# First k-tiles of each later norm multiplied before the token's factor is known (two-layer decoder trunk, one core)

## The chip, the core and the metric

The kernel runs on one core of a Trainium2 chip. Five engines work on their own queues: TensorE (PE, matmuls, with its weight loads shown as PEld), VectorE (DVE), ScalarE (ACT), GpSimd (POOL) and SyncE (SP, which here issues every DMA). The metric is the device time of one execution in microseconds, and each kernel's time is the median of several runs.

## The reference

The model has two layers over 256 tokens of width 2048. Each layer is a mixer and a squared-ReLU MLP. Both begin with an RMS norm that a conditioning vector scales and shifts. Cut to what the change touches:

```python
mod = cond @ ada_w[l] + ada_b[l]
sh1, sc1, g1, sh2, sc2, g2 = [m[:, None, :] for m in jnp.split(mod, 6, axis=-1)]
h = rms_norm(x, norm1_g[l]) * (1.0 + sc1) + sh1
x = x + g1 * mixer(h)                      # layer 0: mLSTM and retention, layer 1: sparse attention
h = rms_norm(x, norm2_g[l]) * (1.0 + sc2) + sh2
x = x + g2 * (jnp.square(jax.nn.relu(h @ mlp_w1[l])) @ mlp_w2[l])
```

`rms_norm` divides each token by the root of the mean of its squares. So for a token t and a weight column, `h @ W` is r[t] times the sum over k of x[t,k] a[k] W[k], plus the sum over k of sh[k] W[k], where r[t] is the token's factor, a = gain x (1 + scale), and the second sum is the same for all tokens.

## The kernel before, in words

Everything is float32 at the ends. Inside, a matmul is made from split operands: `wsplit` rounds a weight tile to `wh` on ACT (line 224) and puts the rest into `wl` on DVE (line 225), and an activation tile `hs` holds its rounded part in columns 0 to 255 and the rest in 256 to 511. One product is then wh x high, wh x rest, wl x high: `tmul` (line 240) does it in two matmuls of 512 and 256 columns, `nmul2` (line 273) in three of 256.

The activations are kept transposed: `xT` has 16 k-tiles of 128 features by 256 tokens. `linear` (line 245) walks over the k-tiles of one group of up to 512 weight columns: for each pair of k-tiles it loads and splits the weights, calls `fill` (below), and multiplies tile by tile into one PSUM bank per entry of its plan; after the last k-tile each entry is evacuated. `residual` (line 455) does the output projections: two groups of eight columns of `xT` each, whose evacuation (line 465, DVE) adds the gated result to `xT[:, k, :]` and tells the next `Norm` with `add(k)`. In the final steps of a group the last `stag` k-tiles are multiplied together, so that the tiles end one after another.

PSUM has eight banks of 512 float32 columns: four in rotation under the name `L` (`lbank`), four single ones M0 to M3 (`bank(i)`). The MLP's first product takes its banks from a rotation over seven (`banks1`), M3 is left to side work. SBUF pools rotate too: 16 `hs` tiles, four each of `raw`, `wh` and `wl`, three `half` tiles of 128x256.

There are four norms. The first is made at the start of the kernel in another way. The three later ones stand at three borders: mixer to MLP in layer 0, MLP to attention input between the layers, attention to MLP in layer 1. There `Norm.add` squares each finished k-tile on ACT (line 419), DVE adds up the first twelve (line 423), and `finish` (line 431) sums over the features with matmuls against ones: the accumulated tile and the last four squares, which gives the sum for every token in all 128 partitions. Then come sqrt (438, ACT), reciprocal (440, DVE) and one Newton step (178 to 180, DVE) over 128x256, and for each of the 16 k-tiles a multiply by the gain column and the factor (447, DVE), the shift with rounding (449, ACT) and the rest (450, DVE). The first matmul behind the border needs the first of these tiles.

Conditioning sums for later norms are worked in beside the matmuls: `Fill(chunks, slots)` has 32 rows of `ada_w` per chunk (line 373 loads one, 375 and 377 multiply and add on DVE) and spreads them evenly over its calls, one per step of `linear`. `side` runs one queued piece of other work per tile.

The order on each engine is made by a list scheduler: the text's order is the priority, an instruction is taken when its inputs and a buffer are there, and `tc.high_priority(offset=n)` moves a block n instructions ahead in priority (60 for the weight splits). On the chip each queue runs in the order that came out.

## Time and profile before

| | us |
|---|---|
| median of 3 runs (lowest, highest) | 2402.22 (2401.34, 2403.44) |
| the profiled execution | 2399.19 |
| its span, first to last instruction | 2397.4 |
| PE busy | 2307.6 (96%) |
| DVE busy | 1720.2 (72%) |
| ACT busy | 1189.9 (50%) |
| POOL busy | 0.5 (0%) |
| mean granted TensorE clock | 0.985 |
| DMA, mean over the span | 255 GB/s |

Rows of a timeline give the start and the length in us, the engine, the line, the operation with output and inputs, and a count; brackets give the idle time of the engine ahead of it and what ended it. Rows of waits give the waiting engine and line, what it waited for, the total, the number of waits and the longest. Rows of groups give busy us and the mean in ns behind the bar. `L124` is the helper that issues every matmul; `L`, `M` in a row are PSUM banks. A granted clock of 0.5 is half speed of PE.

### The profile page before, as it was taken

Reading aid. Unit: us, or ns where it says so; the run is one execution under the profiler, and the core shown is the slowest. Engines: PE = TensorE matmul, PEld = TensorE weight load, DVE = VectorE, ACT = ScalarE, POOL = GpSimd, SP = SyncE. Lnnn points to the kernel's source line nnn. Section 1 sums busy time; section 2 is a strip of 40 time slices with the busy share of each in tenths; the row PEclk is TensorE's granted clock in tenths of the full one; section 3 lists DMA queues with packets and bytes.
Section 4 is the critical chain, followed back from the end, with each engine's and each line's share of the span. In section 5 each row is a group of like instructions: output and inputs, shape, how many; then the busy total and the mean of one; then the engine's idle time right before and its main releaser. Section 6 shows DMA issues by size and latency. Waiting matters only on the chain.

```text
span 2397.4 us, 37302 instructions
## 1 busy us (share of the span) xinstructions
PE 2307.6 (96%) x14101; PEld 2046.1 (85%) x14101; DVE 1720.2 (72%) x2479; ACT 1189.9 (50%) x2205; POOL 0.5 (0%) x8
## 2 busy tenths in 40 slices
PE   5899999999899999999999899999999999999999
PEld 3688889998788888899899799998887888888887
DVE  6768889987877778877877877766676545555545
ACT  3235544444555556555544445755554555544442
POOL 0000000000000000000000000000000000000000
PEclk8999999999999999999999999999999999999999
DMA  9998889988799899888888675444787666565554
GB/s 332 367 291 294 286 292 327 334 295 290 242 322 310 291 316 312 285 307 293 293 311 299 219 254 142 141 140 151 245 307 238 188 184 191 192 193 194 193 193 158
DMA packets 268908, 611.96 MB, mean 255 GB/s; under 512 B 26692, under 2 KB 95286, under 8 KB 268728
## 3 DMA queue, kind: packets, MB, share of 16 engines
q1 hardware_dynamic: 268728, 609.59, 76.6%
q8 instruction: 110, 1.80, 0.3%
q14 instruction: 70, 0.57, 0.1%
HBM read 607.38 MB, written 2.12 MB: 254 GB/s over the span
## 4 chain that ended last, share of the span: by engine, by line
PE 77%; DVE 9%; DMA 9%; issue 3%; ACT 2%; SPq 1%; DVEq 0%; ACTq 0%
PE L L124 46%; PE M L124 30%; DMA ada<-in_ada_w_dram 7%; DVE wl L225 3%; DVE acc L658 1%; DVE acc L377 1%; DMA raw<-in_even_w_in_dram 1%; PE M L317 1%; ACT wh L224 1%; SPq L235 0%; DVE cv L968 0%; ACT junk L320 0%; DVE xT L465 0%; DVE sc L1179 0%; DMA xn<-in_x_dram 0%
## 5 line engine op out<-in xcount | busy, mean ns | idle before, releaser
L124 PE MATMUL L<-hs,wh 128*128 128x256 f32 (+1 forms) x4672 | 1172.8, 328 | 21.1 <-ACT hs L449 7.7
L224 ACT CAST wh<-raw 128x1024 fp32r<-128x1024 f32 (+2 forms) x736 | 765.4, 1042 | 853.6 <-PE M L124 464.0
L225 DVE TENSOR_TENSOR wl<-raw,wh 128x1024 fp32r<-128x1024 f32 (+2 forms) x736 | 887.0, 1211 | 412.9 <-ACT wh L224 402.9
L124 PE MATMUL L<-hs,wl 128*128 128x256 f32 (+1 forms) x3184 | 900.1, 283 | 6.3 <-DVE wl L225 6.2
L124 PEld LDWEIGHTS L<-hs,wh 128*128 128x128 f32 x4672 | 787.0, 191 | 97.7 <-ACT hs L449 8.1
L124 PEld LDWEIGHTS L<-hs,wl 128*128 128x128 f32 (+1 forms) x3184 | 607.2, 191 | 9.3 <-DVE wl L225 7.5
L124 PE MATMUL M<-hs,wh 128*128 128x512 f32 (+2 forms) x1816 | 541.0, 355 | 0.5 <-DVE half L310 0.5
L377 DVE SCALAR_TENSOR_TENSOR acc<-ada,cond,acc 128x1024 f32<-128x1024 f32 x300 | 384.5, 1282 | 149.2 <-DMA ada<-in_ada_w_dram 148.1
L124 PE MATMUL M<-hs,wl 128*128 128x256 f32 (+1 forms) x1476 | 415.2, 281 | 0.0
L124 PEld LDWEIGHTS M<-hs,wh 128*128 128x128 f32 (+1 forms) x1816 | 318.4, 188 | 60.4 <-issue 1.4
L124 PEld LDWEIGHTS M<-hs,wl 128*128 128x128 f32 (+1 forms) x1476 | 278.9, 189 | 1.5 <-issue 0.8
L124 PE MATMUL L<-wh,hs 128*128 128x512 f32 x640 | 210.6, 390 | 0.0
L124 PE MATMUL M<-wh,hs 128*128 128x512 f32 x560 | 185.1, 389 | 0.0
L124 PEld LDWEIGHTS L<-wh,hs 128*128 128x128 f32 x640 | 120.2, 188 | 25.1 <-PE M L124 0.3
L124 PE MATMUL L<-wl,hs 128*128 128x512 f32 x320 | 124.8, 390 | 0.0
L124 PEld LDWEIGHTS M<-wh,hs 128*128 128x128 f32 x560 | 105.1, 188 | 22.0
L124 PE MATMUL M<-wl,hs 128*128 128x512 f32 x280 | 108.9, 389 | 0.0
L320 ACT ACTIVATE junk<-M 128x128 f32<-128x128 f32 x210 | 55.2, 279 | 90.8 <-PE M L317 90.5
L658 DVE SCALAR_TENSOR_TENSOR acc<-ar,cond,acc 128x512 f32<-128x512 f32 x120 | 90.2, 751 | 4.6 <-DMA ar<-in_ada_w_dram 0.9
L556 ACT ACTIVATE half<-half 128x256 f32<-128x256 f32 x128 | 51.5, 413 | 70.7 <-DVE half L310 70.4
L206 ACT CAST hs<-z 128x256 fp32r<-128x256 f32 x192 | 76.2, 400 | 9.7 <-PE L L124 9.7
L207 DVE TENSOR_TENSOR hs<-z,hs 128x256 fp32r<-128x256 f32 x192 | 79.0, 418 | 2.2 <-ACT hs L206 2.2
(247 smaller groups left out, 1299.2 us busy)
## 6 DMA issues: line engine op xcount, KB each, us to landing
raw<-in_mlp_w_dram SPq DMA_DIRECT2D x512, 512.0 KB, 4.5
ada<-in_ada_w_dram SPq DMA_DIRECT2D x320, 512.0 KB, 5.9
raw<-in_even_w_in_dram SPq DMA_DIRECT2D x136, 256.0 KB, 5.5
ar<-in_ada_w_dram SPq DMA_DIRECT2D x64, 512.0 KB, 7.9
raw<-in_odd_w_in_dram SPq DMA_DIRECT2D x48, 512.0 KB, 3.7
raw<-in_even_w_out_dram SPq DMA_DIRECT2D x32, 512.0 KB, 5.8
raw<-in_odd_w_out_dram SPq DMA_DIRECT2D x32, 512.0 KB, 3.7
raw<-in_even_w_in_dram SPq DMA_DIRECT2D x28, 512.0 KB, 5.3
```

The source lines that it names most:

```text
L124: PE.matmul(o, a, b, start=start, stop=stop, skip_group_check=True)
L206: S.copy(h[:, 0:T], src)
L207: V.tensor_tensor(h[:, T:2 * T], src, h[:, 0:T].bitcast(F32), op=OP.subtract)
L224: S.copy(wh[:, :n], raw[:, :n])
L225: V.tensor_tensor(wl[:, :n], raw[:, :n], wh[:, :n].bitcast(F32), op=OP.subtract)
L317: PE.transpose(b[:, i * P:(i + 1) * P], t, ident)
L320: S.activation(j, b[:, i * P:(i + 1) * P], func, accum_out=dst[:, i:i + 1])
L377: V.scalar_tensor_tensor(acc, r, cond[:, kr:kr + 1], acc, op0=OP.mult, op1=OP.add)
L556: S.activation(a, a, AF.Relu)
L658: V.scalar_tensor_tensor(acc, ar[:, kr], cc, acc, op0=OP.mult, op1=OP.add)
```

## The change

At each of the three borders `finish` is replaced. Norm, in `add`, now has DVE sum all 16 squares (and the pool of squares has three tiles instead of five). The stage behind the border begins with a new function `entry`, which takes the place of the first group of the MLP (four tiles of 128 columns, group 0 of 16) or of the first `linear` of attention (key, value, index key and index weight columns).

`entry` first calls `plain`: for the k-tiles 0 to 7 it makes tiles `u` that hold gain times `xT` without the token's factor, split into a high part and a rest, and between them two columns with the high part and the rest of the shift. The `hs` tiles are two columns wider for that. `umul` multiplies such a tile in three matmuls of 258, 256 and 258 columns, so that columns 256 and 257 of the bank collect the shift's products.

`lengths` (priority 600 instructions ahead) gets the token's factor: two matmuls with the accumulated squares as stationary operand and one column of ones give the sums with tokens in partitions, 128x2; sqrt, reciprocal and Newton step run on 128x2; `spread` puts the factor on a diagonal and a matmul with ones brings it to 128x256, which ACT copies to SBUF as `rb`.

The k-tiles 8 to 15 are normed as before (`normed`) and multiplied into two other banks (`late`, two tiles each). After the loop the k-tiles 0 to 7 are normed too, for the groups that follow. Then each of the four tiles is evacuated: the held unscaled sum times `rb` (DVE), the two shift columns added (ACT copy, DVE), and the late sum plus both (DVE). The four held sums are in M0, M1, M2 and an `L` bank in the MLP, in four `L` banks in attention; the late sums in two `L` banks or in M0 and M1.

The slots over which two of the fills are spread change: from 100 to 88 for the first (three chunks, layer 0's mixer), from 100 to 70 for the last (one chunk, layer 1's MLP).

```diff
     def hs_tile():
-        return hsp.tile([P, 2 * T], F32R, tag="hs", name="hs")
+        return hsp.tile([P, 2 * T + 2], F32R, tag="hs", name="hs")
...
+        def plain(self, l, n):
             sh = shift(l, 3 * n)
+            s2 = small.tile([P, 8, 2], F32R, tag="sh2", bufs=1, name="sh2")
+            S.copy(s2[:, :, 0], sh[:, 0:8])
+            V.tensor_tensor(s2[:, :, 1], sh[:, 0:8], s2[:, :, 0].bitcast(F32), op=OP.subtract)
+            us = []
+            for k in range(8):
+                u, a = hs_tile(), acol[:, l, n, k:k + 1]
+                S.activation(u[:, 0:T], xT[:, k, :], AF.Copy, scale=a)
+                S.copy(u[:, T:T + 2], s2[:, k, :].bitcast(F32))
+                V.scalar_tensor_tensor(u[:, T + 2:], xT[:, k, :], a, u[:, 0:T].bitcast(F32), op0=OP.mult, op1=OP.subtract)
+                us.append(u)
+            return us
+
+        def lengths(self):
+            with tc.high_priority(offset=600):
+                b = bank(3)
+                for t in range(2):
+                    mm(b[:, t:t + 1], self.acc[:, t * P:(t + 1) * P], one1, start=t == 0)
+                y, v = st(2, "nv"), st(2, "nw")
+                S.activation(y, b[:, 0:2], AF.Sqrt, scale=1.0 / D, bias=epsc)
+                V.tensor_scalar(v, b[:, 0:2], 1.0 / D, EPS, op0=OP.mult, op1=OP.add)
+                V.reciprocal(y, y)
+                newton(y, v, st(2, "rs_a"))
+                self.rb = tmp.tile([P, T], F32, tag="nm", bufs=1, name="nm")
+                S.copy(self.rb, spread(y, 3))
...
+    def umul(o, u, wh, wl, c, m, start, stop):
+        mm(o[0:m, 0:T + 2], wh[:, c:c + m], u[:, 0:T + 2], start=start, stop=False)
+        mm(o[0:m, 0:T], wh[:, c:c + m], u[:, T + 2:2 * T + 2], start=False, stop=False)
+        mm(o[0:m, 0:T + 2], wl[:, c:c + m], u[:, 0:T + 2], start=False, stop=stop)
+
+    def entry(W, cols, tiles, norm, l, n, held, late, evac, fill):
+        w = sum(b - a for a, b in cols)
+        us = norm.plain(l, n)
+        norm.lengths()
+        hs = [None] * KT
+        for k0 in range(0, KT, 2):
+            if k0 == 8:
+                for k in range(8, KT):
+                    hs[k] = norm.normed(l, n, k)
+            wh, wl = wload(W, k0, 2, cols)
+            fill()
+            for q, (c, m) in enumerate(tiles):
+                for kk in range(2):
+                    k = k0 + kk
+                    if k < 8:
+                        umul(held[q], us[k], wh, wl, kk * w + c, m, k == 0, k == 7)
+                    else:
+                        nmul2(q % 2)(late[q // 2], hs[k], wh, wl, kk * w + c, m, k == 8 and q % 2 == 0, k == KT - 1)
+            side()
+        for k in range(8):
+            hs[k] = norm.normed(l, n, k)
+        for q, (c, m) in enumerate(tiles):
+            b = held[q]
+            t, s = tmp.tile([P, T], F32, tag="half", name="half"), st(1, "shs")
+            V.tensor_tensor(t[0:m], b[0:m, 0:T], norm.rb[0:m], op=OP.mult)
+            S.copy(s[0:m], b[0:m, T:T + 1])
+            V.tensor_tensor(s[0:m], b[0:m, T + 1:T + 2], s[0:m], op=OP.add)
+            evac(q, m, late[q // 2][0:m, q % 2 * T:q % 2 * T + T], s, t)
+        return hs
...
+            def evac_first(q, m, b, s, t):
+                V.scalar_tensor_tensor(t, b, s, t, op0=OP.add, op1=OP.add)
+                squared(q, t)
...
+            hs = entry(io["mlp_w1"][l], [(0, 512)], [(j * P, P) for j in range(4)], before, l, 1,
+                       [bank(0), bank(1), bank(2), lbank()], [lbank(), lbank()], evac_first, fill)
-            for g in range(DFF // 512):
+            for g in range(1, DFF // 512):
...
-        fill = Fill([(0, 2), (0, 3), (0, 4)], 100)
+        fill = Fill([(0, 2), (0, 3), (0, 4)], 88)
...
-    mlp(1, hs, Fill([(1, 5)], 100), None)
+    mlp(1, nrm, Fill([(1, 5)], 70), None)
```

More of the change, by code (lines that the diff above doesn't have):

```diff
@@ L417, in add @@
         def add(self, k):
-            s = tmp.tile([P, T], F32, tag="sq", bufs=5, name="sq")
+            s = tmp.tile([P, T], F32, tag="sq", bufs=3, name="sq")
             S.activation(s, xT[:, k, :], AF.Square)
@@ L421, in add @@
                 V.tensor_copy(self.acc, s)
-            elif self.n < KT - 4:
+            else:
                 V.tensor_tensor(self.acc, self.acc, s, op=OP.add)
-            else:
-                self.last.append(s)
             if self.n == 9:
@@ L429, in add @@
             self.n += 1
-        def finish(self, l, n):
-            b = bank()
-            mm(b[:, 0:T], ones, self.acc, start=True, stop=False)
-            for i, s in enumerate(self.last):
-                mm(b[:, 0:T], ones, s, start=False, stop=i == len(self.last) - 1)
-            y = tmp.tile([P, T], F32, tag="nm", bufs=1, name="nm")
-            v, a = (tmp.tile([P, T], F32, tag="sq", bufs=5, name="sq") for _ in range(2))
-            S.activation(y, b[:, 0:T], AF.Sqrt, scale=1.0 / D, bias=epsc)
-            V.tensor_scalar(v, b[:, 0:T], 1.0 / D, EPS, op0=OP.mult, op1=OP.add)
-            V.reciprocal(y, y)
-            newton(y, v, a)
-            rb = y
-            sh = shift(l, 3 * n)
-            hs = []
-            for k in range(KT):
-                t = tmp.tile([P, T], F32, tag="half", name="half")
-                V.scalar_tensor_tensor(t, xT[:, k, :], acol[:, l, n, k:k + 1], rb, op0=OP.mult, op1=OP.mult)
-                h = hs_tile()
-                S.activation(h[:, 0:T], t, AF.Identity, bias=sh[:, k:k + 1])
-                V.scalar_tensor_tensor(h[:, T:2 * T], t, sh[:, k:k + 1], h[:, 0:T].bitcast(F32),
-                                       op0=OP.add, op1=OP.subtract)
-                hs.append(h)
-            return hs
@@ new lines, in normed @@
+        def normed(self, l, n, k):
+            t = tmp.tile([P, T], F32, tag="half", name="half")
+            V.scalar_tensor_tensor(t, xT[:, k, :], acol[:, l, n, k:k + 1], self.rb, op0=OP.mult, op1=OP.mult)
+            h, sh = hs_tile(), shift(l, 3 * n)
+            S.activation(h[:, 0:T], t, AF.Identity, bias=sh[:, k:k + 1])
+            V.scalar_tensor_tensor(h[:, T:2 * T], t, sh[:, k:k + 1], h[:, 0:T].bitcast(F32),
+                                   op0=OP.add, op1=OP.subtract)
+            return h
@@ L534, in result, with mlp @@
                 SP.dma_start(out[0, t * P:(t + 1) * P, c * 512:(c + 1) * 512], o)
-    def mlp(l, hs, fill, norm):
+    def mlp(l, before, fill, norm):
         with ExitStack() as es:
@@ L1077, in tile_trunk @@
     mixs.close()
-    hs = nrm.finish(0, 1)
-    nrm = Norm()
-    mlp(0, hs, Fill([(0, 5), (1, 0), (1, 1), (1, 3), (1, 4)], 256), nrm)
+    before, nrm = nrm, Norm()
+    mlp(0, before, Fill([(0, 5), (1, 0), (1, 1), (1, 3), (1, 4)], 256), nrm)
     fill = Fill([(1, 2)], 60)
-    hs = nrm.finish(1, 0)
     wO = io["odd_w_in"][0]
@@ L1134, in evac_s, with evac_in @@
                 V.tensor_scalar(iw.rearrange("p a b -> p (a b)"), tb[:, 0:32], 0.25 * 0.125, None, op0=OP.mult)
-        linear(wO, KT, 2, [(2048, 2304), (3328, 3392), (3328, 3408)], hget_ := (lambda k: hs[k]),
-               [[(0, P), (P, P)], [(2 * P, P), (3 * P, 16)]], evac_s, lambda j: lbank(), fill=fill)
+        def evac_in(q, m, b, s, t):
+            V.scalar_tensor_tensor((kT, vT, ik, iwT)[q], b, s[0:m], t[0:m], op0=OP.add, op1=OP.add)
+            if q % 2:
+                evac_s(q // 2)
+        hs = entry(wO, [(2048, 2304), (3328, 3392), (3328, 3408)], [(0, P), (P, P), (2 * P, P), (3 * P, 16)],
+                   nrm, 1, 0, [lbank() for _ in range(4)], [bank(0), bank(1)], evac_in, fill)
+        hget_ = lambda k: hs[k]
         sc1 = ap.tile([P, T], F32, name="sc1")
```

18 lines of the change are left out of this document (8 added, 10 removed).

## The prediction

> **What bounds the kernel now.** I read the page's busy table first, then the waits with TensorE (PE) as the waiting engine, then the stretches around the three later norms, then the timeline there. PE is busy 96% of the span, so only what PE loses counts; ScalarE (ACT) and VectorE (DVE) matter where PE waits for them.
>
> ```profile
> PE 2307.6 (96%) x14101; PEld 2046.1 (85%) x14101; DVE 1720.2 (72%) x2479; ACT 1189.9 (50%) x2205; POOL 0.5 (0%) x8
> ...
> PE L L124 <- ACT hs L449: 7.7, 1, 7.7
> PE L L124 <- DVE hs L450: 5.7, 2, 5.0
> PE M L317 <- DVE acc L377: 5.3, 1, 5.3
> ```
>
> Two of these waits are on the normed tiles `hs` of `finish`, the third (a conditioning sum) lies inside the first border and hides the norm behind it. In stretches cut at the last residual matmul and the first matmul of the next stage (columns: length, busy time and count of PE, weight load, DVE, ACT, POOL, granted clock, DMA share, GB/s):
>
> ```profile
> 596.71:609.20 12.49, 4.66 (x19) 2.89 (x18) 12.49 (x19) 5.92 (x17) 0.00 (x0) 0.71 0.80 259
> 609.20:612.50 3.30, 3.30 (x11) 2.83 (x12) 3.30 (x9) 2.42 (x12) 0.00 (x0) 0.53 0.67 256
> 1342.27:1354.82 12.55, 3.58 (x14) 1.76 (x13) 12.08 (x22) 3.92 (x10) 0.00 (x0) 0.79 0.58 178
> 1354.82:1360.00 5.18, 5.18 (x24) 4.69 (x25) 5.18 (x14) 3.04 (x8) 0.00 (x0) 0.52 1.09 369
> 1656.14:1665.54 9.40, 3.45 (x19) 2.42 (x18) 9.21 (x15) 4.88 (x10) 0.00 (x0) 0.90 0.63 209
> 1665.54:1670.50 4.96, 4.96 (x15) 4.28 (x16) 4.96 (x13) 3.22 (x8) 0.00 (x0) 0.51 0.07 29
> ```
>
> I call the borders A (mixer to MLP, layer 0), B (MLP to attention input) and C (attention to MLP, layer 1). Each costs its gap and then a stretch at half the granted clock, in which (1 - clock) of the length is lost: A 12.49 + 3.30 x 0.47 = 14.0, B 12.55 + 5.18 x 0.48 = 15.0, C 9.40 + 4.96 x 0.49 = 11.8, together **40.9 us**. That is the most the borders can give back. DVE is busy for the whole of A's gap, 12.08 of 12.55 us at B and 9.21 of 9.40 at C; this decides the rest.
>
> The Trainium skill, "TensorE: Matmul & The Clock Gate", section "Part 1: The HAM clock gate", has PE fall to half speed after an idle window of about 3.4 us and need some 3.4 us of work to leave it. By it a resume would cost 1.7 us, 5.1 for three, and a wait below its window nothing beyond itself. A's 3.30 us agrees, B's 5.18 and C's 4.96 are longer, and the row at 587.29 below is a wait of 1.79 us that is followed by 3.30 us at clock 0.50, which goes against the window.
>
> **The change part by part.** A's timeline, PE's last residual products first:
>
> ```profile
> 595.83 0.40 PE L124 MATMUL L<-hs,wh 128*128 128x256 f32 x2
> 596.19 0.40 PE L124 MATMUL L<-hs,wh 128*128 128x256 f32 x2
> 596.43 0.28 PE L124 MATMUL L<-hs,wl 128*128 128x256 f32 x1
> 597.30 0.87 DVE L465 SCALAR_TENSOR_TENSOR xT<-L,mod,xT 128x256 f32<-128x256 f32 x2
> 600.68 1.74 DVE L440 RECIPROCAL nm<-nm 128x256 f32<-128x256 f32 x1
> 603.42 0.41 DVE L178 TENSOR_TENSOR sq<-nm 128x256 f32<-128x256 f32 x1
> 603.75 1.28 DVE L377 SCALAR_TENSOR_TENSOR acc<-ada,cond,acc 128x1024 f32<-128x1024 f32 x1
> 604.95 0.42 DVE L179 SCALAR_TENSOR_TENSOR sq<-sq 128x256 f32<-128x256 f32 x1
> 607.48 1.27 DVE L447 SCALAR_TENSOR_TENSOR half<-xT,acol,nm 128x256 f32<-128x256 f32 x3
> 609.20 0.79 PE L124 MATMUL L<-hs,wh 128*128 128x512 f32 x1 [0.65 <-DVE hs L450]
> ```
>
> *Removed:* the last eight squares no longer go into PE's sums (they did so in its idle time, so nothing is won), and the chain of sqrt, reciprocal and Newton step over 128x256 gives way to one over 128x2. *Added to PE:* eight k-tiles of unscaled products, 4 tiles each, three matmuls of 258, 256 and 258 columns per tile; nearest is the three-matmul form above, 0.36 us (595.83 to 596.19). These need only the first half of xT, which is final half a residual earlier, so PE can start at once: 8 x 4 x 0.36 = 11.5 us of work. The other eight follow, 23.0 us in all.
>
> ```profile
> 560.00:596.71 36.71, 34.92 (x278) 34.72 (x277) 26.52 (x30) 13.70 (x18) 0.00 (x0) 0.95 0.88 300
> 1300.00:1342.27 42.27, 42.27 (x271) 37.89 (x270) 26.11 (x33) 17.01 (x35) 0.00 (x0) 1.00 0.84 267
> 1620.00:1656.14 36.14, 36.14 (x303) 36.14 (x302) 17.52 (x21) 15.05 (x19) 0.00 (x0) 1.00 0.59 180
> L449 ACT ACTIVATE hs<-half,mod 128x256 fp32r<-128x256 f32 x48 | 21.1, 498 | 15.9 <-DVE half L447 15.8
> ```
>
> *Making the unscaled tiles:* eight multiply-subtracts on DVE (0.48 us each by the 128x256 rows below, 3.8 us) and on ACT eight scalings (0.50 us by L449's 128x256 row, 4 us) and eight two-column copies. DVE has 10 to 18 us free ahead of each border, ACT over 20, and the old tiles' buffers come free while the residual runs, so I cost this at nothing; without that cover it is 3.8 us of DVE per border.
>
> *The token's factor.* Five 128x2 steps and two 128x128 diagonal ones: 5 x 0.16 + 2 x 0.28 = 1.4 us of DVE, with a matmul and copies between. By estimate the squares and sums behind the last xT (598.2 at A) take 1.5 us (two of 0.42 each way, and the hand-over) and this chain 4; another DVE operation of 1.2 us can slip between its steps, as L377 does above. The factor stands between 5.5 and 10 us after PE's last residual product, bounds from no slip and from four; both are below 11.5, so PE has its first eight k-tiles and the wait that opened the borders goes.
>
> ```profile
> L178 DVE TENSOR_TENSOR rs_a<-hf 128x2 f32<-128x2 f32 (+1 forms) x51 | 7.7, 157 | 0.6
> L196 DVE TENSOR_SCALAR diag<-c,hf x2: 280/283/286, 1388.7 to 1388.9; 128x128 f32<-128x128 f32 x2
> L310 DVE TENSOR_TENSOR half<-L,half 128x256 f32<-128x256 f32 x74 | 31.0, 420 | 5.2 <-ACT half L309 3.7
> L465 DVE SCALAR_TENSOR_TENSOR xT<-L,mod,xT 128x256 f32<-128x256 f32 x48 | 21.1, 477 | 4.3 <-PE L L124 4.3
> 623.98 3.49 DVE L225 TENSOR_TENSOR wl<-raw,wh 128x1024 fp32r<-128x1024 f32 x3
> 1342.91 2.04 DVE L465 SCALAR_TENSOR_TENSOR xT<-M,mod,xT 128x256 f32<-128x256 f32 x5
> 1353.74 1.28 DVE L447 SCALAR_TENSOR_TENSOR half<-xT,acol,nm 128x256 f32<-128x256 f32 x3
> 1366.02 0.97 DVE L225 TENSOR_TENSOR wl<-raw,wh 128x800 fp32r<-128x800 f32 x1
> 1367.19 0.48 DVE L450 SCALAR_TENSOR_TENSOR hs<-half,mod,hs 128x256 fp32r<-128x256 f32 x1 [0.19 <-ACT hs L449]
> ```
>
> *What is late next.* `entry` holds four PSUM banks for the unscaled sums and two for the late ones, and lets them go only in its evacuations, which stand behind all sixteen `normed` tiles and share their three `half` buffers. Before, the next group found three free banks; now an MLP finds one and attention, which needs an `L` bank, none. So PE stops at the end of the first group until DVE has come through its list. From B's rows sixteen normed tiles take 1353.74 to 1367.67 less 0.97 and 0.19: **12.8 us**. A weight split is 3.49 / 3 = 1.16 us, the narrow one 0.97. An MLP tile's evacuation is 0.42 + 0.16 + 0.48 = 1.06 us of DVE, and a bank pair needs two. Fill rows due in the eight steps are 5.0, 4.4 and 3.8 (steps times 160/254, 32/58, 32/68); I let 3, 3 and 2 of them come ahead, at 1.28. DVE's list from PE's last residual product:
> A: last xT 0.9, two sums 0.8, factor 1.4, nine splits 10.5 (seven here, two of the next group), normed 12.8, fill 3.8, two evacuations 2.1 = 32.3 us.
> B: xT 2.4, four sums 1.7, factor 1.4, splits 7 x 0.97 + 1.2 = 8.0, normed 12.8, fill 3.8, one held bank 0.6 = 30.7.
> C: as A with two fill rows: 31.1.
> PE has 23.0 us of work, at A and C also the first tile of the next group for two steps (1.4): it waits 7.9, 7.7 and 6.7 us, and I add 2.0 for the half clock after each, the middle of the losses above (1.55 to 2.49). Lost after: 9.9 + 9.7 + 8.7 = 28.3 instead of 40.9, a gain of **12.6 us**. Bounds: all 40.9 if evacuations slip in early; a loss, if the list is longer (below).
>
> *The fill rates.* The first goes from 100 to 88 slots, so the sums of the second shift and scale are due 12 steps earlier and leave the end of the mixer's residual, where this stands:
>
> ```profile
> 587.29 0.39 PE L124 MATMUL L<-hs,wl 128*128 128x256 f32 x1 [1.79 <-DVE wl L225]
> 588.38 1.28 DVE L377 SCALAR_TENSOR_TENSOR acc<-ada,cond,acc 128x1024 f32<-128x1024 f32 x1 [1.15 <-DMA ada<-in_ada_w_dram]
> 588.40:591.70 3.30, 3.30 (x18) 3.30 (x18) 3.30 (x5) 0.47 (x2) 0.00 (x0) 0.50 0.82 302
> 350.00:400.00 50.00, 48.92 (x397) 47.85 (x396) 44.30 (x77) 27.06 (x52) 0.00 (x0) 1.00 1.00 336
> ada<-in_ada_w_dram SPq DMA_DIRECT2D x320, 512.0 KB, 5.9
> DVE acc L377 <- DMA ada<-in_ada_w_dram: 148.1, 132, 4.9
> ```
>
> The 1.79 us wait and the half clock behind it (3.30 x 0.50) cost 3.4 us; such a wait can return elsewhere on the same in-order queue, so I take half, 1.7. The last fill, 100 to 70 slots, lies in a stage with DMA to spare (209 GB/s and less); bounds of half a microsecond either way, taken as 0. The wider tile and the three-matmul form change PE's pace by nothing that the rows tell apart.
>
> **Sum.** The profiled execution is 2399.19 us, 1.8 above its span and 3.0 below the runs' median of 2402.22. 2399.19 - 12.6 - 1.7 = 2384.9; with 3.0 for the median 2387.9, rounded to **2388 us** (0.6% less).
>
> **The rivals.**
> 1. *Nothing takes the wait's place.* If the first evacuations run between the normed tiles, banks come free in time and all 40.9 + 1.7 goes: 2402.2 - 42.6 = 2360. For it: DVE's queue is planned by readiness, not by text alone (L377 between Newton's steps). Against: all evacuations come last in the text, and DVE has no free time until then.
> 2. *The faster first fill crowds the transfers of layer 0.* Twelve rows of 0.524 MB move ahead, 6.3 MB, 18.7 us at the 336 GB/s of 350 to 400, where the DMA share is already 1.00. DVE waits for these rows (148.1 us in all) with weight splits behind them. Were two thirds of it PE's, 12.5 us, the gain is gone: 2400. Against: 560 to 597 ran at a share of 0.88, so there is room where the rows no longer are.
> 3. *Slower: DVE's list ahead of the evacuations is longer than the old gap.* The change puts PE's wait behind every DVE operation of the border. If the unscaled tiles aren't made ahead (3.8), all fill rows come (2 more, 2.6) and each arrives late by the mean wait of 148.1 / 132 = 1.1 (4 to 5 rows, 5), the list grows by 11.4 us at each border: 3 x 11.4 = 34.2 against a gain of 12.6, so 2402.2 + 21.6 - 1.7 = 2422. It decides from 12.6 / 3 = 4.2 us more per border than I counted, a list of 36.5 us at A. For it: DVE has no free time in the gaps now. Against: it has before them.
>
> **How the numbers follow.** My forecast has a chance of 0.51 (2376 to 2397 by itself: the waits 4 us shorter or 3 longer each), rival 1 with 0.20, rival 2 with 0.17, rival 3 with 0.12. A measurement here can tell about 0.2%, 4.8 us, from no change. The forecast and rival 1 are faster, 0.71; rival 2 is the same, 0.17; rival 3 slower, 0.12. The range 2360 to 2405 leaves out most of rival 3 and the lower half of rival 1's own spread.
>
> **What would show it.** Right: no wait of PE on `hs` at the three borders and the granted clock at 1.0 through the last residual product and 23 us on; the 128x2 reciprocal within 7 us of that product; then PE waiting for a DVE evacuation of `entry` at the end of the first group, 7 to 8 us each, with half clock after it; no wait at 585. Wrong: evacuations among the normed tiles and PE running on (rival 1); new waits of PE on weight splits between 300 and 540 (rival 2); DVE lists above 36 us (rival 3); or PE waiting at once for the unscaled tiles, which I priced at nothing.

## The result and the profile after

The changed kernel takes **2382.71 us** in the median of four runs (2381.23 to 2386.11) against 2401.78 us for the one before on the same chip (2399.16 to 2403.44): a ratio of **0.9925**, 95% interval 0.9906 to 0.9943. It is faster, by 0.75%; 2388 was forecast. Its profiled execution took 2383.08 us with a span of 2381.3, 16.1 us less than that of before. The sum was nearly right by luck, since its terms were not: the borders gave 6.1 us more than forecast, the wider tile took 8.8 us at the end and gave some 6.6 on the way, and the faster fill gave nothing of its 1.7. The ratios in this document leave out one execution alone, of 4462.27 us, a slow one among the twelve of `b_chain`.

The busy table after, and the kinds of wait with PE as the waiting engine (total us, number, longest, over the whole kernel) that occur in the stretches behind the borders. Of the 9.5 us on `wl`, only 1.9 lie there, and of the 1.6 on `junk`, 1.2:

```profile
PE 2303.3 (97%) x14217; PEld 2039.1 (86%) x14217; DVE 1727.0 (73%) x2550; ACT 1202.5 (50%) x2263; POOL 0.5 (0%) x8
```

```profile
PE L L124 <- DVE wl L225: 9.5, 8, 4.1
...
PE L L124 <- DVE shs L500: 3.2, 1, 3.2
...
PE M L124 <- DVE wl L225: 2.4, 1, 2.4
PE M L317 <- ACT junk L320: 1.6, 2, 1.2
PE M L124 <- ACT hs L462: 1.5, 1, 1.5
...
PE L L124 <- DVE hs L463: 0.8, 1, 0.8
...
PE M L124 <- DVE shs L500: 0.7, 1, 0.7
```

The three waits of before (7.7 and 5.7 us on normed tiles, 5.3 on a conditioning sum) are gone. In their place stand shorter ones: on weight splits (`wl`), on the column sums' bank (`junk`), on the factor's first tile (`hs`) and, as forecast, on the evacuation of the held tiles (`shs`). Here they are in the timeline, A first, then B, then C; the bracket is the wait ahead of the row:

```profile
601.84 0.39 PE L124 MATMUL M<-hs,wl 128*128 128x258 f32 x1 [2.40 <-DVE wl L225]
612.69 0.67 PE L124 MATMUL M<-diag,c 128*128 128x256 f32 x2 [0.19 <-DVE diag L196]
613.84 0.66 PE L317 MATMUL M<-c,acc 128*128 128x128 f32 x4 [0.47 <-ACT nm L456]
615.72 0.97 PE L317 MATMUL M<-c,acc 128*128 128x128 f32 x4 [1.23 <-ACT junk L320]
632.77 0.43 PE L124 MATMUL L<-hs,wl 128*128 128x256 f32 x1 [1.91 <-DVE wl L225]
1355.09 1.03 PE L124 MATMUL M<-hs,wh 128*128 128x256 f32 x3 [1.52 <-ACT hs L462]
1371.79 0.47 PE L124 MATMUL L<-hs,wh 128*128 128x256 f32 x2 [3.16 <-DVE shs L500]
1671.05 0.51 PE L124 MATMUL L<-hs,wh 128*128 128x512 f32 x1 [0.81 <-DVE hs L463]
1673.37 0.50 PE L124 MATMUL M<-hs,wh 128*128 128x512 f32 x1 [0.66 <-DVE shs L500]
```

And the stretches in which the granted clock (the column behind POOL) shows what came with them:

```profile
596.30:613.00 16.70, 14.12 (x103) 13.69 (x101) 13.65 (x25) 8.23 (x12) 0.00 (x0) 0.90 0.77 251
613.00:620.00 7.00, 5.29 (x29) 4.70 (x28) 6.96 (x15) 5.38 (x24) 0.00 (x0) 0.76 0.90 303
620.00:646.00 26.00, 24.09 (x154) 21.86 (x153) 23.34 (x44) 15.79 (x30) 0.00 (x0) 0.93 0.51 154
1352.80:1359.90 7.10, 5.43 (x28) 4.34 (x27) 5.89 (x15) 4.52 (x9) 0.00 (x0) 0.77 1.04 339
1656.50:1670.00 13.50, 13.50 (x111) 13.16 (x109) 13.50 (x29) 9.66 (x16) 0.00 (x0) 1.00 0.45 133
```

Counted as in the prediction (waits, and 1 - clock of a stretch), the borders now lose: A 2.40 + 0.19 + 0.47 + 1.23 + 1.91 = 6.2 of waits and 16.7 x 0.10 + 7.0 x 0.24 + 26.0 x 0.07 = 5.2 of clock, 11.4; B 1.52 + 3.16 and 7.1 x 0.23 = 1.6, 6.3; C 1.5. Together **19.2 us** instead of 40.9.

Where the time went can be followed more exactly, since both kernels push the same 4,500,480 columns through PE in products of weights and activations (the two extra columns not counted). The table takes PE's work done by a moment of the kernel before (first row, us) and says how many us earlier the other kernel's profiled execution had done as much. It holds the experiments too, which are told below. Each row is one execution. How far single executions differ can be read from `a_swap`, `a_fill2`, `a_hz` and `a_hz2`, in which PE, DVE and ACT run the changed kernel's instructions in the same order up to 1400 us: their leads at 645 run from 0.6 to 8.3 us, and what the stretch from 590 to 645 wins from 1.0 to 4.3. What B and C win repeats better, 6.7 to 7.1 and 10.5 to 10.6.

```
before at     400   590   612   645  1000  1335  1356  1385  1645  1690  1830  1960  2380
changed      -6.3  -0.4  14.5   0.6  -0.7   2.1  15.6   9.2  12.0  22.6  26.2  24.9  16.1
a_fill1      -0.1   2.5  17.4   7.9   0.1   2.7  16.3   9.9  12.5  23.1  23.9  22.7  13.8
a_fill2      -5.0   4.0  18.9   8.3   6.6   9.6  23.2  16.4  19.1  29.6  34.1  32.8  23.9
b_wide       -1.7  -0.8  -0.9  -1.4  -2.0   1.7   1.7   1.4   2.7   3.6   7.5   6.3  -2.6
a_swap      -10.0  -0.1  14.8   2.4   0.1   2.3  15.8   9.0  12.0  22.6  25.8  24.5  15.7
a_hz         -8.1   0.9  15.8   3.5   2.6   5.3  18.8  12.0  14.8  25.3  31.2  30.0  18.0
a_hz2        -2.2   1.9  16.8   4.2   4.2   5.6  19.2  12.7  15.0  25.6  30.2  28.9  28.2
b_chain      -2.3  -1.7  -6.8  -7.4 -13.0 -12.8 -14.3 -16.0 -16.9 -18.2 -17.0 -17.0 -16.9
a_evac_first -11.4 -7.9   7.0  -8.9  -8.8  -7.9   5.7  -2.7   1.3  11.9  13.5  12.3   3.4
a_light      -8.5  -2.7  12.2   1.8  -0.7   1.1  14.6  12.5  15.2  25.8  33.6  32.4  23.5
a_hz2_pool   -9.2  -1.8  13.1  -5.3  -5.3  -2.8  10.8  -4.5  -1.3   9.3  12.4  11.2  10.5
a_late_fill  -8.8  -2.3  12.6   1.3  -0.3   2.2  15.8   7.9  10.6  21.2  27.2  25.9  17.1
a_gate       -8.7   5.1  20.0   6.4  -1.4  -0.7  12.9   5.2   8.1  18.7  23.3  22.1  13.2
```

Border A wins 14.9 us by 612 and has given them back by 645, all but 1.0 (up to 4.3 in the other four). B wins 7.1 (2.1 to 9.2), C 10.6 (12.0 to 22.6). Between the borders the kernel creeps ahead (1.5 from 645 to 1335, 2.8 from 1385 to 1645, 2.3 from 1690 to 1960), and then, in the last projection, where nothing was meant to change, it **loses 8.8 us**. PE waits for nothing there and the granted clock is 1.00; each product simply takes longer. The kernel before and the changed one, groups of that stretch (busy us and mean ns of one behind the bar):

```profile
L124 PE MATMUL M<-wh,hs 128*128 128x512 f32 x440 | 144.4, 389 | 0.0
```

```profile
L124 PE MATMUL M<-wh,hs 128*128 128x512 f32 x432 | 143.8, 394 | 0.0
```

Both are from the same 300 us (2060 to 2360): 440 products against 432. From start to start it is 226.9 ns before and 231.8 after.

### The profile page after: what moved, and what is told of

It reads as the page before. It is cut to its first block, busy times and chain, and to the rows that moved or that the text cites. A ratio compares the mean times of both kernels' runs of the same rounds, so it can differ in the third digit from the quotient of the medians.

```text
span 2381.3 us, 37638 instructions
## 1 busy us (share of the span) xinstructions
PE 2303.3 (97%) x14217; PEld 2039.1 (86%) x14217; DVE 1727.0 (73%) x2550; ACT 1202.5 (50%) x2263; POOL 0.5 (0%) x8
## 4 chain that ended last, share of the span: by engine, by line
PE 73%; DVE 13%; DMA 8%; issue 3%; ACT 2%; SPq 1%; DVEq 0%; ACTq 0%
PE L L124 42%; PE M L124 30%; DMA ada<-in_ada_w_dram 4%; DVE wl L225 4%; DMA raw<-in_even_w_in_dram 3%; DVE acc L716 2%; DVE acc L377 2%; ACT wh L224 1%; PE M L317 1%; DMA ar<-in_ada_w_dram 1%; DVE hs L463 1%; DVE half L460 1%; DVE cv L1026 0%; SPq L235 0%; DVE hs L207 0%
## 5 line engine op out<-in xcount | busy, mean ns | idle before, releaser
L124 PE MATMUL L<-hs,wh 128*128 128x256 f32 (+2 forms) x4704 | 1154.5, 324 | 7.2 <-DVE shs L500 3.2
L124 PEld LDWEIGHTS L<-hs,wl 128*128 128x128 f32 x3168 | 599.5, 189 | 14.1 <-DVE wl L225 11.0
L124 PE MATMUL M<-hs,wh 128*128 128x256 f32 (+3 forms) x1912 | 547.3, 348 | 3.4 <-ACT hs L462 1.5
L124 PE MATMUL M<-hs,wl 128*128 128x256 f32 (+2 forms) x1492 | 420.2, 282 | 2.4 <-DVE wl L225 2.4
L124 PEld LDWEIGHTS M<-hs,wh 128*128 128x128 f32 (+1 forms) x1912 | 331.3, 188 | 60.8 <-ACT hs L462 1.9
L206 ACT CAST hs<-z 128x256 fp32r<-128x256 f32 x192 | 76.3, 401 | 10.6 <-PE M L124 10.6
```

The costliest lines, as they stand in the source:

```text
L124: PE.matmul(o, a, b, start=start, stop=stop, skip_group_check=True)
L206: S.copy(h[:, 0:T], src)
```

## The experiments

### The last projection: the wide tile

In the last projection the activation tile `hs` is the stationary operand and the weights stream past it. The change made `hs` 514 columns wide, and its 16 tiles moved from 2048 to 2080 bytes apart. Theory: this spacing makes the products slower. Rivals: another part of the change, or the weight tiles, which the wider pool pushed along. First the wide tile alone, in the kernel before (`b_wide`):

```diff
-        return hsp.tile([P, 2 * T], F32R, tag="hs", name="hs")
+        return hsp.tile([P, 2 * T + 2], F32R, tag="hs", name="hs")
...
-            s = tmp.tile([P, T], F32, tag="sq", bufs=5, name="sq")
+            s = tmp.tile([P, T], F32, tag="sq", bufs=4, name="sq")
...
```

> The kernel before with nothing changed but the width of the hs tiles (514 columns instead of 512, so that the tiles lie 2080 bytes apart and the weight buffers 512 bytes further on; the pool of squares has four tiles instead of five to make room). Layout theory: the last projection, whose 128x512 matmuls took 389 ns before and 395 after the change, takes 395 ns here too and the kernel is 8 to 9 us slower than before. Rival (the slower matmuls come from the changed schedule or from the chip's state): 389 ns and no change of time, within 4 us.

Measured: 2403.12 us, ratio 1.0005 (0.9989 to 1.0021), no change in time. But its last projection runs at 231.8 ns, as the changed kernel's, and loses 8.9 us there (6.3 to -2.6), after the same kernel had come 7.5 us ahead by 1830. So the wide tile has two effects that cancel here: it slows the products in which `hs` is stationary and quickens those in which it streams. In the second MLP product of layer 0 (1000 to 1330 us) the 512-column products go from 237.0 ns start to start before to 232.9 in the changed kernel.

The weights' place was undone by putting their pool ahead of the `hs` pool (`a_swap`):

```diff
-    hsp = ctx.enter_context(tc.tile_pool(name="hsp", bufs=16))
     wp = ctx.enter_context(tc.tile_pool(name="wp", bufs=4))
     tmp = ctx.enter_context(tc.tile_pool(name="tmp", bufs=3))
+    hsp = ctx.enter_context(tc.tile_pool(name="hsp", bufs=16))
```

> The changed kernel with the weight pool placed in front of the hs pool, which puts the weight buffers on the same offsets within 4096 bytes as in the kernel before, while the hs tiles keep their 2080 bytes. If the offset of the weight buffers costs the last projection its 2%: 389 ns and 8 to 9 us faster than the changed kernel, about 2374 us. If the spacing of the hs tiles does: 395 ns and 2383 us. If neither: 395 ns and 2383 us here, and 389 ns in the kernel before with wide tiles.

Measured: 2383.47 us, ratio 0.9917 (0.9887 to 0.9946), still 231.9 ns and 8.8 us lost. It is not the weights' place. Next, three tiles of 2048 bytes for the last projection alone (`a_hz`):

```diff
...
-                result(io["mlp_w2"][l], lambda k: split_to_hs(z[k]))
+                hz = es.enter_context(tc.tile_pool(name="hz", bufs=3))
+                result(io["mlp_w2"][l], lambda k: split_to_hs(z[k], hz.tile([P, 2 * T], F32R, tag="hz", name="hz")))
```

> The changed kernel, but the last projection splits its activations into three tiles of 512 columns of their own (2048 bytes apart) instead of the pool of 514-column tiles (2080 bytes apart). Theory 1 (the spacing of the stationary tiles slows the 512-column products): one of the 128x512 rows of the last 400 us falls from 394 to about 389 ns, start to start from 232-233 to 227 ns, the last projection loses under 1 us against the kernel before instead of 8.5, and the time is 2383 - 8.5 = about 2374 us (2370 to 2378). Rival (something else in the changed kernel's last stage, such as the weights' place or the order of the splits, slows it): 232 ns stays and the time is 2383 us; with only three tiles the splits could also come late, which would show as waits of PE on the split tiles, and the time would be over 2385 us.

Measured: 2385.88 us, ratio 0.9929 (0.9907 to 0.9952). The theory as stated fell: the tiles are 2048 bytes apart again, and the products are slower still, 234.3 ns from start to start, with 12.0 us lost. Its group in the same 300 us:

```profile
L124 PE MATMUL M<-wh,hz 128*128 128x512 f32 x425 | 142.7, 396 | 0.0
```

The changed kernel's trace, sorted by the tile, told why. The tiles there step by 32 bytes in their start modulo 256, and so the 64 k-tiles of the last projection repeat a pattern of eight. Mean ns from start to start of the `wh` products, the step to the next k-tile not counted, by the start of the stationary tile modulo 256 (the weight tiles start at 224 in all of these kernels, as did every `hs` tile before; the starts are those of the kernel's memory plan, the traces hold no addresses):

```
start mod 256     0     32     64     96    128    160    192    224
ns            233.4  233.5  234.1  233.2  231.5  227.6  233.2  227.5
```

The `wl` products, which the table leaves out, take 228.0 ns at 224 but 231.7 at 160, so over all products 224 alone keeps the old pace. This suggested that not the distance but the start counts, and `a_hz` had all of its tiles at 64, the worst of the table. Its three tiles were then moved by 160 bytes, to 224 (`a_hz2`, against `a_hz`):

```diff
+                pad = es.enter_context(tc.tile_pool(name="pad", bufs=1))
+                G.memset(pad.tile([P, 40], F32, name="pad"), 0.0)
                 hz = es.enter_context(tc.tile_pool(name="hz", bufs=3))
```

> The same as the kernel with three 512-column tiles of their own in the last projection, but with a pad of 160 bytes ahead of them, so that each starts at 224 bytes over a multiple of 256, as the weight tiles do and as all tiles of the kernel before did (there they started at 64 over). Theory (what counts is where the stationary tile starts against 256 bytes: in the changed kernel the mean start to start goes 228, 233, 229, 233, 233, 234, 233, 233 ns over every eight k-tiles, whose starts step by 32 bytes, and it was 234 for all at 64 over): 227 ns for all, the last projection loses under 1.5 us against the kernel before, and the time is 8 to 9 us below the changed kernel, 2373 to 2377 us. Rival (the number of tiles or their being a pool of their own slows it): 234 ns again and 2383 to 2386 us.

Measured: **2372.18 us**, ratio **0.9886** (0.9864 to 0.9908), the fastest kernel of this study that computes the whole reference. 226.5 ns from start to start, 0.7 us lost in the last projection, and the group is back at 389:

```profile
L124 PE MATMUL M<-wh,hz 128*128 128x512 f32 x443 | 145.5, 389 | 0.0
```

What follows: 160 bytes are worth 10 to 11 us here (10.3 by the ratios of `a_hz` and `a_hz2`, 12.0 - 0.7 = 11.3 by equal work). That the start of the stationary tile sets the pace is shown; what in the hardware makes it so isn't.

### The fills

Each fill's rate was set back alone, the first (`a_fill1`), then the last (`a_fill2`):

```diff
-        fill = Fill([(0, 2), (0, 3), (0, 4)], 88)
+        fill = Fill([(0, 2), (0, 3), (0, 4)], 100)
```

> The changed kernel with the first fill back at 100 slots. By equal work the changed kernel falls 4 to 6 us behind the one before between 380 and 510 us and is level again at the first border. Theory that the denser fill crowds the transfers there: here it stays within 2 us of the kernel before between 380 and 510 us, and reaches the first border up to 3 us earlier; total 2380 to 2383 us. Rival (the denser fill clears the rows ahead of the first border and earns what it costs): the same lead lost again by the first border, total 2383 us or more.

```diff
-    mlp(1, nrm, Fill([(1, 5)], 70), None)
+    mlp(1, nrm, Fill([(1, 5)], 100), None)
```

> The changed kernel with the last fill back at 100 slots. By equal work the changed kernel wins some 3 us in the last MLP's first product beyond what the border gave. Theory that this is the last fill's: here the total is 2 to 4 us more, 2385 to 2387 us, with the waits of TensorE on evacuations and weight splits of that stage (1.7 and 2.3 us before) back. Rival: no change, 2383 us.

Measured: 2384.26 us, ratio 0.9917 (0.9888 to 0.9946), and 2386.08 us, 0.9912 (0.9878 to 0.9945): neither differs from the changed kernel. The table shows what the first rate does: with 88 slots the kernel is 5 to 11 us behind at 400 in every variant but one, and in all but `a_evac_first` it has caught up to within 3 us at 590; with 100 it isn't behind at either. This is a loss in the place where rival 2 had it, half of its 12.5 us in the changed kernel (6.3), but it is a loan, paid back before the border. That the rate makes it is shown; that it comes from crowded transfers isn't, since from 350 to 400 the changed kernel's DMA share is 0.95 at 309 GB/s, against 1.00 at 336 before. The last rate moves nothing that can be told: `a_fill2` gains 3.2 us from 1690 to 1960 with the old rate, the changed kernel 2.3 with the new one. `a_fill2`'s profiled run was one of its quicker ones (2375.18 in runs from 2371.65 to 2386.87), ahead from 560 us on, so its absolute numbers aren't to be read.

### The borders: the chain for the factor

In `b_chain` the kernel before gets the new chain for the factor, with everything normed in the old order and no unscaled tiles:

```diff
         def finish(self, l, n):
-            b = bank()
-            mm(b[:, 0:T], ones, self.acc, start=True, stop=False)
...
+            self.lengths()
+            return [self.normed(l, n, k) for k in range(KT)]
```

> The kernel before with the new chain for the token's factor alone (squares summed on DVE, two one-column products, four operations on two columns, the spread, all at the raised priority), but no unscaled tiles: PE still stands from the residual's end to the first normed tiles. Theory (the time comes from the eight unscaled k-tiles that fill the gap, the shorter chain is worth a part): each of the three gaps shrinks from about 12.5, 12.5 and 9.4 us to 7 to 9 us, which is worth 9 to 13 us in all less what is given back behind the first border; 2389 to 2397 us. Rival 1 (the chain alone makes the whole gain): 2383 us or less. Rival 2 (the gap is set by late evacuations and what DVE does between, not by the chain's operations): gaps unchanged, 2400 to 2404 us. The tiles here are 512 columns wide, so the last projection should keep 227 ns from start to start.

Measured: 2411.6 us, ratio **1.0039** (1.0022 to 1.0055): slower than before. No expectation had that; rival 2 came nearest. Its waits at A (590 to 640 us):

```profile
PE M L124 <- DVE diag L196: 5.5, 1, 5.5
PE M L124 <- DVE ssq L423: 5.3, 1, 5.3
PE L L124 <- DVE hs L447: 3.7, 1, 3.7
```

From the last evacuation into `xT` to the first normed tile DVE takes 9.8, 9.3 and 7.2 us before (A, B, C), 13.7, 10.4 and 7.9 here, and 12.8, 11.2 and 8.3 in the changed kernel. The chain has shorter operations, but more hand-overs: all 16 squares go through DVE, then PE, ACT, DVE, PE and ACT take turns, and at each turn another operation slips in ahead. DVE's timeline of the changed kernel at A, where a reciprocal and three steps of 0.16 us each take 4.5 us:

```profile
602.03 0.48 DVE L514 SCALAR_TENSOR_TENSOR xT<-L,mod,xT 128x256 f32<-128x256 f32 x1
...
606.53 0.16 DVE L453 RECIPROCAL nv<-nv 128x2 f32<-128x2 f32 x1
606.60 1.21 DVE L225 TENSOR_TENSOR wl<-raw,wh 128x1024 fp32r<-128x1024 f32 x1
607.72 0.16 DVE L178 TENSOR_TENSOR rs_a<-nv 128x2 f32<-128x2 f32 x1
608.45 1.23 DVE L225 TENSOR_TENSOR wl<-raw,wh 128x1024 fp32r<-128x1024 f32 x1 [0.57 <-ACT wh L224]
609.59 0.15 DVE L179 SCALAR_TENSOR_TENSOR rs_a<-rs_a,nw 128x2 f32<-128x2 f32 x1
609.66 1.28 DVE L377 SCALAR_TENSOR_TENSOR acc<-ada,cond,acc 128x1024 f32<-128x1024 f32 x1
610.86 0.15 DVE L180 SCALAR_TENSOR_TENSOR nv<-rs_a,nv 128x2 f32<-128x2 f32 x1
```

So the new chain by itself is a loss, and the gain of the change rests on the unscaled k-tiles. What the chain costs inside the changed kernel isn't shown, as no run has the unscaled tiles with the old chain. Nor is all of `b_chain`'s loss at the borders: 10.2 us by the table (5.7, 3.2 and 1.3), and 5.6 from 645 to 1000 (its profiled execution, 2416.18, is one of its slower ones).

### The borders: VectorE's list and the banks

The forecast held that DVE's list ahead of the evacuations makes PE wait for banks. `a_evac_first` puts the evacuations ahead of the first eight normed tiles:

```diff
-        for k in range(8):
-            hs[k] = norm.normed(l, n, k)
         for q, (c, m) in enumerate(tiles):
             b = held[q]
...
             evac(q, m, late[q // 2][0:m, q % 2 * T:q % 2 * T + T], s, t)
+        for k in range(8):
+            hs[k] = norm.normed(l, n, k)
```

> The changed kernel, with the four evacuations of each entry's held tiles put ahead of making the first eight normed tiles. Theory (the prediction's step, DVE's list holds the banks): the second border's wait of 3.2 us on the evacuation's sum and the third's of 0.7 go with the half clock behind them, the kernel is 4 to 6 us further ahead of the one before at the end of the second border than the changed kernel is (9 to 15 us instead of 9), and the time is 2376 to 2380 us. Rival (the wait only moves: the next group then waits for the first eight normed tiles, four evacuations later): no gain beyond 1 us at the second border, 2382 to 2385 us. The first border, which showed no such wait, should not change in either.

Measured: 2390.81 us, ratio 0.9951 (0.9931 to 0.997), some 6 us worse than the changed kernel by the ratios and more than theory or rival had. The wait does move, as the rival had it: in its waits from 610 to 650 us there is now

```profile
PE L L124 <- DVE hs L463: 4.9, 1, 4.9
```

and A, from 590 to 645, loses 1.0 us where five executions of the old order won 1.0 to 4.3; B wins 5.2 us (-7.9 to -2.7) where it won 6.7 to 7.1. The 7.5 us by which this execution is behind the changed kernel at 590 aren't the edit's: up to 620 us PE, DVE and ACT run the same order in both, and waits differ between executions (this one, 2395.74, is one of the slower of its seven). Next, the changed kernel's order with a shorter list (`a_light`). It leaves the token's factor out of the first eight normed tiles, so it doesn't compute the reference and shows a price only:

```diff
+            if k < 8:
+                S.activation(h[:, 0:T], xT[:, k, :], AF.Identity, scale=a, bias=sh[:, k:k + 1])
+                V.scalar_tensor_tensor(h[:, T:2 * T], xT[:, k, :], a, h[:, 0:T].bitcast(F32), op0=OP.mult, op1=OP.subtract)
+                return h
...
```

> The changed kernel with less work for VectorE in each entry: the first eight normed tiles, used from the second group on, leave out the token's factor (and the low part leaves out the shift), so that VectorE makes each with one operation instead of two: 8 x 0.42 to 0.48 = 3.4 to 3.8 us off its list per border; ScalarE, TensorE and all transfers have the same work. Theory (VectorE's list sets when the held tiles are evacuated and the weight splits come, the prediction's step): the second border's wait of 3.2 us on the evacuation falls to under 0.7 and with the half clock behind it 3 to 5 us are won there; at the first border the waits of 1.9 us on a weight split at 630 us and 0.5 to 2 us more are won, and the third wins under 1 us: 2374 to 2379 us. Rival (the evacuations wait for ScalarE's copies or for TensorE's order and not for VectorE's list): the 3.2 us stays within 0.7 and the time is 2381 to 2386 us.

Measured: 2375.61 us, ratio 0.9876 (0.9856 to 0.9896). At B the evacuation's wait falls from 3.16 to 0.3; A's wait of 1.91 us at 632 and C's two are gone. B's waits in this kernel (1340 to 1400 us):

```profile
PE M L124 <- ACT hs L467: 1.5, 1, 1.5
PE M L124 <- DVE diag L196: 0.4, 1, 0.4
PE L L124 <- DVE shs L505: 0.3, 1, 0.3
```

B now wins 11.4 us (1.1 to 12.5), 4.3 more than in the changed kernel, with eight operations fewer on DVE. In the changed kernel DVE is busy without a gap from 1364.43 until PE goes on at 1371.79, so the wait isn't one for ACT's copies. That DVE's list sets the bank wait at B is thereby shown. The same relief without leaving anything out (`a_hz2_pool`, on top of `a_hz2`) gives the multiplication to GpSimd:

```diff
+            if k < 8:
+                S.activation(t, xT[:, k, :], AF.Copy, scale=acol[:, l, n, k:k + 1])
+                G.tensor_tensor(t, t, self.rb, op=OP.mult)
...
```

> The kernel with aligned tiles of their own in the last projection (2372 us), with the same relief for VectorE but nothing left out: for the first eight normed tiles ScalarE scales the residual (eight operations of about 0.5 us per border more) and GpSimd, which is idle in this kernel, multiplies by the factor. Theory (VectorE's list bounds, and GpSimd's product is short enough to hide behind the entry's last steps): the second border's wait on the evacuation falls by over 2 us and the time is 2365 to 2370 us. Rival A (GpSimd's product, which no trace here has shown, takes several us, eight in a row come after the second group wants its tiles): waits on the normed tiles of over 2 us at each border and 2374 to 2390 us. Rival B (ScalarE's extra operations delay the high parts and splits as much as VectorE gains): 2371 to 2374 us.

Measured: 2391.88 us, ratio 0.9948 (0.9929 to 0.9968), 0.006 worse than `a_hz2`. This is rival A's mechanism: GpSimd takes 1.13 us for the product alone where DVE took 0.48 for gain and factor together, eight in a row hold up DVE's last step and with it the evacuations, and at B PE waits 9.0 us. The rival had the waits on the normed tiles at each border (they are 3.3 us at A, none at B and 1.4 at C) and a time up to 2390. GpSimd's group in this kernel, and the wait from 1340 to 1400 us:

```profile
L462 POOL TENSOR_TENSOR half<-half,nm 128x256 f32<-128x256 f32 x24 | 26.9, 1133 | 1133.9 <-ACT half L461 837.6 <-DVE wl L225 296.3
```

```profile
PE L L124 <- DVE shs L504: 9.0, 1, 9.0
```

### Border A: who takes the gain back

At A the waits aren't on banks. Rows of the next fill and their column sums stand there, so the first guess was that they take the gain. `a_late_fill` calls that fill 24 steps later:

```diff
-                       [bank(0), bank(1), bank(2), lbank()], [lbank(), lbank()], evac_first, fill)
+                       [bank(0), bank(1), bank(2), lbank()], [lbank(), lbank()], evac_first,
+                       fill if l else lambda: None)
...
-                       [[(j * P, P)] for j in range(4)], evac, banks1, fill=fill)
+                       [[(j * P, P)] for j in range(4)], evac, banks1, fill=fill if l or g > 2 else None)
...
-    mlp(0, before, Fill([(0, 5), (1, 0), (1, 1), (1, 3), (1, 4)], 256), nrm)
+    mlp(0, before, Fill([(0, 5), (1, 0), (1, 1), (1, 3), (1, 4)], 232), nrm)
```

> The changed kernel, with the layer-0 MLP's conditioning rows started 24 steps later (none in the entry or in groups 1 and 2, 232 steps for the rest), so that neither their multiply-adds nor their column sums stand in the first border. Theory (the first border's gain, 14.5 us at 612 us, is given back by 645 us to those rows: PE waits for weight splits behind them and for their column sums' bank, each followed by half clock): at 645 us the kernel is 8 to 13 us ahead of the one before instead of 0.6, and if nothing eats it later, the time is 2371 to 2376 us. Rival A (the waits come from DVE's norm tiles and evacuations, which stand there in any case): under 4 us at 645 us and 2381 to 2385 us. Rival B (the denser rows later, 0.69 a step instead of 0.62, cost what the border gains): ahead at 645 us, level by 900 to 1300 us, 2381 to 2390 us.

Measured: 2385.06 us, ratio 0.9927 (0.99 to 0.9955), 1.3 us ahead at 645. This decides nothing, because the edit didn't move the rows: their first still begins at 529 us (526 in the changed kernel) and the column sums still stand at 614. The scheduler takes a row as soon as its buffer is free and DVE has nothing else, wherever the text puts it. `a_gate` holds them by data instead, through the two buffers that the sums need:

```diff
         norm.lengths()
+        if hasattr(fill, "held"):
+            for _ in range(2):
+                g = wp.tile([P, 1024], F32, tag="acc", bufs=2, name="acc")
+                V.tensor_copy(g[:, 0:2], norm.rb[:, 0:2])
```

> The changed kernel with the first conditioning rows of the next fill held back to the factor of the first border: both of the sums' two buffers are written once, two columns, from the spread factor before the first row may use them. The rows that the changed kernel's VectorE took up from 526 us on, through the first border, then begin behind the factor, and the column sums that stood at 614 us come later. Theory (rows and their column sums in the first border cost what is given back between 612 and 645 us): the waits on weight splits at 599 and 630 us and on the column sums' bank at 613 us go, the kernel is 8 to 13 us ahead of the one before at 645 us instead of 0.6, and if the delayed rows hide in the layer-0 MLP the time is 2371 to 2376 us. Rival A (VectorE's own list of normed tiles, evacuations and weight splits makes the waits): under 4 us ahead at 645 us and 2381 to 2385 us. Rival B (the rows that are late pile up behind the border): ahead at 645 us, level again by 900 us, 2381 to 2388 us.

Measured: 2387.52 us, ratio 0.9938 (0.992 to 0.9957). Now the first row begins at 602 and the sums stand at 677; the kernel is 5.1 us ahead at 590 and 20.0 at 612, and has 6.4 left at 645 and none at 1000. Its waits from 590 to 650 us, now mostly on normed tiles:

```profile
PE L L124 <- DVE hs L463: 5.2, 3, 4.2
PE L L124 <- DVE wl L225: 2.4, 1, 2.4
```

From 590 to 645 the gain is 1.3 us, within the 1.0 to 4.3 with the rows in place, so the theory fell. Rival B came: the lead is lost by 1000, 7.8 us of it after 645, where the changed kernel loses 1.3. Rival A's waits on DVE's own list are there, though the lead at 645 is over its 4 us. DVE's groups in the changed kernel from the first unscaled product at A to the first evacuation:

```profile
L225 DVE TENSOR_TENSOR wl<-raw,wh 128x1024 fp32r<-128x1024 f32 x10 | 12.2, 1220 | 1.8 <-ACT wh L224 1.8
L460 DVE SCALAR_TENSOR_TENSOR half<-xT,acol,nm 128x256 f32<-128x256 f32 x16 | 6.8, 480 | 0.0
L463 DVE SCALAR_TENSOR_TENSOR hs<-half,mod,hs 128x256 fp32r<-128x256 f32 x16 | 6.8, 479 | 0.0
L377 DVE SCALAR_TENSOR_TENSOR acc<-ada,cond,acc 128x1024 f32<-128x1024 f32 x3 | 3.8, 1281 | 1.1 <-DMA ada<-in_ada_w_dram 1.1
```

These four are 29.6 us of DVE's work, 3.8 of it rows. What stays open is how the some 10 us that A still loses divide between waits and clock: in `a_light` the splits' wait at 632 is gone too (0.3 us is left), and A wins 4.5 (-2.7 to 1.8), 0.2 more than the best of the five executions above.

## Why the prediction was right, and where it was wrong

- **The first eight k-tiles fill the gap, their tiles made ahead at no cost: right.** The unscaled products begin at 596.15, 1339.96 and 1643.75 us with no wait on their tiles at any border, and `b_chain` shows that without them there is no gain. Of the signs that I gave, no wait on `hs` at all held at A alone: the normed tiles behind the first eight were waited for at B (1.52) and C (0.81).
- **Each gap was counted as lost whole: too much.** The rows at the gaps have PE busy for 4.66, 3.58 and 3.45 us of them. The `ssq` and `sq` products went, but the column sums, the spread and C's transposes remain and now stand in PE's way: the count gives 40.9 - 19.2 = 21.7 us, the table at equal work 1.0 + 7.1 + 10.6 = 18.7 (19.8 to 21.6 in the other four executions of the same order).
- **The factor stands 5.5 to 10 us after the last residual product: wrong at A and B, the upper bound at C.** The spread factor was copied at 613.41, 1353.60 and 1653.74, which is 17.3, 13.6 and 10.0 us behind the first unscaled product, and this follows the last residual product at once. I bounded it by no slip and by four; at A eight operations of about 1.2 us stand between the last evacuation into `xT` and the first normed tile. It cost little, since the eight k-tiles last 12.8 to 16.1 us: a wait of 1.52 at B.
- **PE then waits 7.9, 7.7 and 6.7 us for banks at the end of the first group: right in kind, wrong in size, and at A in place.** It was none, 3.16 and 0.66. The lists were sized well: from the first unscaled product to the first evacuation's shift sum (line 500) DVE took 31.5 us at B and 29.4 at C (forecast to the release 30.7 and 31.1). PE came to the bank later than I had it, 28.7 and 29.0 us instead of 23.0 and 24.4, with the small products, one wait and B's half clock between; and at C one evacuation freed a bank where I had asked for two. At A the list took 36.5 us, and PE lost its time ahead of it, piece by piece, to splits, sums and clock.
- **2.0 us of half clock after each wait:** 5.2 at A, 1.6 at B, none at C.
- **The faster first fill clears the wait at 585, 1.7 us: wrong reading.** The rows there were those of the next fill, taken up far ahead of their place in the text: its first row begins at 540 us in the kernel before. `a_fill1` and the changed kernel end alike. The last fill at 0 was right.
- **The wider tile changes nothing that rows tell apart: this is the step that failed outright.** It costs 8.8 us in the last projection and wins some in the stages where `hs` streams (1.5 + 2.8 + 2.3 = 6.6 between the borders and behind them; in `b_wide`, without the rest of the change, 3.1, 1.3 and 2.7). That the price of nothing came out 2 us off is because the two cancel.

So the borders gave 18.7 where 12.6 was forecast, the stretches between them 6.6 and the last projection -8.8 where 0 was, and the first fill -0.4 where 1.7 was: 16.1 us in all against 14.3. That these errors cancel is luck. Rival 1's condition, evacuations among the normed tiles early enough to free the banks in time, didn't come about; rival 2's loss did, and was paid back; rival 3's long list was met at A, 36.5 us, its own threshold, and there the border won little (1.0 to 4.3 us), though not by a wait on banks.

## What to carry to other kernels

Filling a dependency gap of PE with work that doesn't need the late value pays, but the work of the other engines that used to stand in that gap doesn't go away: count VectorE's whole list from the old gap to the next point at which PE needs its result, and look for what PE meets first. Before a tile gets two columns wider, look at where the following tiles then start: keep stationary tiles on the starts that they had, or give a stage its own tiles there, as `a_hz2` does. And to hold back work that a list scheduler may take early, give it a dependency; its place in the text doesn't hold it.

## What the runs showed of the hardware

The pace of products of 512 columns depends on where the stationary tile starts modulo 256 bytes, with the weights at 224, a granted clock of 1.00 and no waits: 226.5 to 228.0 ns from start to start at 224, 227.6 (`wh`) and 231.7 (`wl`) at 160, 231.5 to 237.1 at the other six multiples of 32. Where the activations stream and the weights stand, tiles that all start at 224 were the slower ones (237.0 in the kernel before, a mean of 232.9 over all starts in the changed kernel). No run shows the cause.

The length of a wait doesn't say whether half clock follows. B in the changed kernel, stretches at its two waits:

```profile
1353.50:1355.09 1.59, 0.07 (x1) 0.00 (x1) 1.08 (x3) 0.93 (x3) 0.00 (x0) 1.00 1.14 309
1355.09:1358.30 3.21, 3.06 (x17) 2.86 (x18) 3.21 (x9) 2.92 (x7) 0.00 (x0) 0.74 1.09 358
1358.30:1361.00 2.70, 2.70 (x18) 2.28 (x18) 2.70 (x6) 1.68 (x3) 0.00 (x0) 0.68 0.55 210
...
1368.60:1371.79 3.19, 0.03 (x2) 0.03 (x1) 3.19 (x11) 2.52 (x7) 0.00 (x0) 1.00 0.49 159
1371.79:1375.00 3.21, 3.21 (x27) 3.21 (x28) 3.07 (x8) 0.31 (x2) 0.00 (x0) 1.00 0.30 61
```

After 1.59 us of standstill the clock is 0.74 and 0.68 for 5.9 us, after 3.19 us it stays at 1.00. The Trainium skill, "TensorE: Matmul & The Clock Gate", section "Part 1: The HAM clock gate", has the clock halve after an idle window of about 3.4 us: the wait of 3.19 us agrees, the one of 1.59 us doesn't.
